# Seven products instead of eight in some block pairs of a gate and up projection, with the middle activations turned through device memory

## The chip, the cores and the metric

The kernel is one launch on one core of a Trainium2 chip. The metric is device time in microseconds, the median of several runs of the whole kernel. The engines that matter here are TensorE (PE in the profile; its weight loads are listed as PEld), VectorE (DVE), ScalarE (ACT), GpSimd (POOL) and SyncE (SP), which only issues DMAs.

## The reference

One layer of a decoder trunk on 256 tokens of width 2048, with 16 learned tokens ahead of them, in float32. The layer is a half-step FFN, a mixer of sparse attention and a gated short convolution, and a second half-step FFN, which is the part that is changed:

```python
def swiglu(x, w_gate, w_up, w_down):
    return (jax.nn.silu(x @ w_gate) * (x @ w_up)) @ w_down
...
        u = rms_norm(h, ffn2_norm_g[l])
        h = h + 0.5 * swiglu(u, ffn2_w_gate[l], ffn2_w_up[l], ffn2_w_down[l])
```

`w_gate` and `w_up` are 2048 x 5632, `w_down` is 5632 x 2048. The result is the 256 tokens without the learned ones.

## The kernel before

**Precision.** Every float32 operand of a large matmul is split into a rounded part (hi) and the rest (lo), and a product is three matmuls: hi·hi, hi·lo, lo·hi. The activations are split once and stay on chip (`act`, `mid`). Each weight is read once from device memory and split on the way.

**The stream.** `Stream` (L66 to L158) runs through all weights of the kernel in the order in which they are used. A chunk is 128 x 2048 floats, 1 MB; SyncE loads it into one of three `raw` buffers (L100). `split` (L106) cuts a chunk into subs of 1024 columns, here two blocks of 128 x 512. For each sub ACT copies `raw` to `whi` (L115) and VectorE subtracts to get `wlo` (L116). There are four buffers of each, and splits are issued three subs ahead of the one in use, so the split of a sub waits for the matmuls of the fourth sub before it. `next` (L137), called by the matmul code for each sub, first issues the split that is due, and then the steps that other code has put off with `later(fn, lag)`: these run in order of their due sub. So the order of instructions on ACT and VectorE is written out by hand, counted in subs. Each engine takes its instructions in that order.

**The second FFN.** `ffn_tokens` (L487) keeps tokens as the output rows: 128 tokens (index `j`, 1 or 2) by 512 columns is one accumulator bank. The 5632 middle columns are 11 slices of 512, in two groups of 6 and 5 (`GROUPS`). For each slice `f`:

- `tokens` (L308) makes the gate: 16 blocks of weights (`k`), two per sub, for both `j`, three matmuls each (L316 to L318): 8 subs of 12 matmuls of 128x512. Then the same for up: 192 matmuls in all.
- `gate` (L505) is Silu on ACT from the accumulator, with the norm's scale of each token; `times` (L509) multiplies by the up half on VectorE.
- `turn_columns` (L478) turns the 256 tokens x 512 columns so that columns lie on partitions: per call four VectorE transposes of 32 partitions x 256 (L389), four calls per slice, 16 transposes. A 32x32 block is turned in place by one transpose; taking a source and a target on different partitions moves the block.
- `split_into` (L339) writes hi and lo of the turned slice to `mid`.

After a group's slices come four output blocks `pd` of 512 columns each, with `mid` as activations, and `add` (L515) adds them to the residual.

Ahead of the second FFN the output projection of the mixer (`po`) makes the new residual in four quarters `g`. `add_out` (L1045) adds and squares, `turn_columns` turns, and `to_act` (L1056) scales, and splits into `act`. The last quarter falls into the first subs of the second FFN: its 16 transposes come two calls to a sub there (`per`), then `to_act`.

Of the kernel before, what the change touches and what calls it, by code (L numbers as in the profile page):

```python
# [23 lines left out]
META = 16  # L24
# [37 lines left out]
PITCH = 5 * LINE  # L62
LATER = LINE - META
SUB = 1024
RAW = 2048


class Stream:
# [7 lines left out]
    def __init__(self, nc, raw_pool, split_pool):  # L76
        self.nc, self.raw_pool, self.split_pool = nc, raw_pool, split_pool
        self.loads, self.subs = [], []
        self.raw, self.ready = {}, {}
        self.n_loaded = self.n_split = self.at = 0  # L80
        self.blocks, self.waiting, self.steps = [], [], []
        self.first = []

    def add(self, src, n, width, cuts=()):

# [20 lines left out]
    def split(self, upto):  # L106
        nc = self.nc
        while self.n_split < min(upto, len(self.subs)):
            g, c, kk, width = self.subs[self.n_split]
            self.load(g + RAW_BUFS)  # L110
            n = kk * width
            raw = self.raw[g][:, c : c + n]
            hi = self.split_pool.tile([P, SUB], F32R, name="whi")
            lo = self.split_pool.tile([P, SUB], F32R, name="wlo")
            nc.scalar.activation(hi[:, :n], raw, AF.Copy)  # L115
            nc.vector.tensor_sub(lo[:, :n], raw, hi[:, :n].bitcast(F32))  # L116
# [4 lines left out]
            if self.n_split == len(self.subs) or self.subs[self.n_split][0] > g:  # L121
                self.load(g + 1 + RAW_BUFS)

    def later(self, fn, lag=1, least=0):

# [36 lines left out]
def tile_decoder_layer(  # L162
# [22 lines left out]
    nc = tc.nc  # L185
# [26 lines left out]
    chunks(wo, 0, KD, 512)  # L212
    gu = down = 0
    for n in GROUPS:
        chunks(wgu2, gu, gu + 8 * n, 512)
        chunks(wd2, down, down + 4 * n, 512)
        gu, down = gu + 8 * n, down + 4 * n

# [53 lines left out]
    def mm_tile(name="mm"):  # L272
        return psum.tile([P, 512], F32, name=name, tag="mm")
# [34 lines left out]
    def tokens(ps_of, x, n):  # L308

        k = 0  # L310
        while k < n:
            blocks = [st.next()] + st.rest()
            for j, ps in ps_of.items():
                for i, (whi, wlo) in enumerate(blocks):
                    xhi, xlo = x(k + i, j, 0), x(k + i, j, 1)
                    nc.tensor.matmul(ps, xhi, whi, start=k + i == 0, stop=False)  # L316
                    nc.tensor.matmul(ps, xhi, wlo, start=False, stop=False)  # L317
                    nc.tensor.matmul(ps, xlo, whi, start=False, stop=k + i == n - 1)  # L318
            k += len(blocks)

    def act_tokens(k, j, part):
        t0, n = TT[j]
# [155 lines left out]
    def turn_columns(mt, s, r):  # L478

        for q in range(4):  # L480
            turned(
                mt.rearrange("p f (j r b) -> p r j f b", j=2, r=4)[:, r],
                s.rearrange("p j (f q b) -> p q j f b", f=4, q=4)[:, q],
                q, r,
            )

    def ffn_tokens():  # L487

        with tc.tile_pool(name="ffn2", bufs=1, reuse_waits="tile") as fp:
            mid = fp.tile([P, 4 * GROUPS[0], 2, SEQ], F32R, name="mid")  # L490

            late["junk"] = lambda: fp.tile([P, 512], F32, name="junk")
            late["mt"] = lambda: fp.tile([P, 4, SEQ], F32, name="mt", bufs=2)
            root, inverse = rsqrt(rcol[:, 0, :2], sums[:, 0], (P, 2), 1.0 / D)

            def add_up():
                for g in (0, 2):
                    nc.vector.tensor_add(sums[:, g], sums[:, g], sums[:, g + 1])
# [6 lines left out]
            def gate(pg, s):  # L505
                for j in (1, 2):
                    nc.scalar.activation(s[:, j - 1], pg[j], AF.Silu, scale=rcol[:, 0, j - 1 : j])

            def times(pu, s):  # L509
                for j in (1, 2):  # L510
                    nc.vector.scalar_tensor_tensor(
                        s[:, j - 1], pu[j], rcol[:, 0, j - 1 : j], s[:, j - 1], op0=ALU.mult, op1=ALU.mult
                    )

            def add(d, j, pd, last):  # L515
                to = ht[d][:, j - 1]
                nc.vector.scalar_tensor_tensor(to, pd, 0.5, to, op0=ALU.mult, op1=ALU.add)
                if last:
                    queue = nc.gpsimd if st.n_loaded < len(st.loads) else (nc.sync, nc.scalar)[j - 1]
                    queue.dma_start(out[j - 1, :, d * 512 : (d + 1) * 512], to)  # L520

            for c, n in enumerate(GROUPS):
                for f in range(n):
                    s = fp.tile([P, 2, 512], F32, name="s", bufs=2)
                    mt = fp.tile([P, 4, SEQ], F32, name="mt", bufs=2)
                    pg = {j: mm_tile(f"pg{j}") for j in (1, 2)}
                    tokens(pg, act_tokens, KD)
                    st.later(lambda pg=pg, s=s: gate(pg, s))
                    pu = {j: mm_tile(f"pu{j}") for j in (1, 2)}
                    tokens(pu, act_tokens, KD)  # L530
                    st.later(lambda pu=pu, s=s: times(pu, s))
                    for r in range(4):
                        st.later(lambda mt=mt, s=s, r=r: turn_columns(mt, s, r), 2 + r)
                    to = mid[:, 4 * f : 4 * f + 4]
                    st.later(lambda to=to, mt=mt: split_into(to[:, :, 0], to[:, :, 1], mt), 6)
# [27 lines left out]
    late = {}  # L563
    with ExitStack() as mix:
# [491 lines left out]
        def to_act(g, mt):  # L1056
            for f in range(4):
                d = 4 * g + f
                hi, lo = (act[:, d, i, LATER + META :][:, :SEQ] for i in range(2))
                gain = gains[2][:, d : d + 1]  # L1060
                nc.scalar.activation(hi, mt[:, f], AF.Copy, scale=gain)
                nc.vector.scalar_tensor_tensor(
                    lo, mt[:, f], gain, hi.bitcast(F32), op0=ALU.mult, op1=ALU.subtract
                )
# [12 lines left out]

# [67 lines left out]
def _layout(x, meta_tokens, ffn1_norm_g, ffn1_w_gate, ffn1_w_up, ffn1_w_down, mix_norm_g, w_in, q_norm_g,  # L1145
# [32 lines left out]
    gu = np.stack([_tiles(ffn2_w_gate[0], 512), _tiles(ffn2_w_up[0], 512)], 1)  # L1178
    a["wgu2"] = _chunks(gu.reshape(-1, P, KD * 512))
    a["wd2"] = _down_columns(ffn2_w_down[0])  # L1180
    return a

# [18 lines left out]
```

## Time and profile before

| | |
|---|---|
| median of 3 runs | 2143.2 us (2143.09 to 2143.22) |
| span of the profiled execution | 2141.4 us |
| first and last gate matmul of the second FFN start at | 1419.0 and 2006.4 us |
| busy: TensorE, VectorE, ACT, GpSimd | 2136.3, 1325.8, 954.5, 10.0 us |
| read from device memory | 393.49 MB |

The span runs from the first to the last instruction of one profiled execution; the runs' times are whole executions, and the profiled one's own time is known by its span alone. A row of instructions reads: source line, engine, operation, output <- inputs, shapes, count, then busy time and mean duration of one in ns, then the time in which the engine stood idle just before them and what ended it. A row of the timeline reads: start, duration, engine, line, operation, and in brackets the idle time before it. Matmuls are pipelined, so the duration of one is longer than the distance to the next.

### The profile page before, as it was taken

How to read it: one execution, taken by the hardware profiler on the slowest of the kernel's cores; microseconds unless marked ns; L12 is line 12 of the kernel's file. 1: busy time of each engine (PE TensorE's matmuls, PEld its weight loads, DVE VectorE, ACT ScalarE, POOL GpSimd, SP SyncE). 2: the span in 40 equal slices, each digit the busy share in tenths (PEclk: the TensorE clock that was granted, in tenths of full speed). 3: DMA queues.
4: the chain of work that ended last, by engine and by line, in shares of the span. 5: the costliest groups of instructions: out<-in, count | busy, mean ns of one | idle time of the engine just before them, and what ended most of it. 6: DMA issues, size and time to landing. Idle time of an engine off the chain costs nothing.

```text
span 2141.4 us, 30929 instructions
## 1 busy us (share of the span) xinstructions
PE 2136.3 (100%) x12902; PEld 1921.2 (90%) x12902; DVE 1325.8 (62%) x1776; ACT 954.5 (45%) x1173; POOL 10.0 (0%) x28
## 2 busy tenths in 40 slices
PE   9999999999999999999999999999999999999999
PEld 9999999999999998799988888888888888888887
DVE  7555544455555556677686487886676644666664
ACT  6444433344444445565444444454444433444442
POOL 0000000000000000000000000000000000000000
PEclk9999999999999999999999999999999999999999
DMA  7555545555544545454555555555555555555554
GB/s 267 189 181 179 179 180 178 178 177 177 177 178 178 177 170 177 159 176 158 172 188 194 194 189 204 177 183 210 196 196 186 196 191 195 196 197 195 189 200 143
DMA packets 56909, 397.58 MB, mean 186 GB/s; under 512 B 6337, under 2 KB 7105, under 8 KB 9409
## 3 DMA queue, kind: packets, MB, share of 16 engines
q1 hardware_dynamic: 55872, 393.51, 53.4%
q8 instruction: 101, 1.65, 0.3%
q10 hardware_dynamic: 576, 1.05, 0.1%
q0 software_dynamic: 320, 1.05, 0.1%
q14 instruction: 40, 0.32, 0.0%
HBM read 393.49 MB, written 2.10 MB: 185 GB/s over the span
## 4 chain that ended last, share of the span: by engine, by line
PE 99%; DMA 0%; DVE 0%; SPq 0%; ACT 0%; issue 0%; ACTq 0%
PE pd L290 4%; PE pd L289 4%; PE pd L288 4%; PE pu L289 4%; PE pg L289 4%; PE pg L288 4%; PE pu L288 4%; PE pu L290 4%; PE pg L290 4%; PE pg L317 4%; PE pg L318 4%; PE pd L318 4%; PE pu L317 4%; PE pg L316 4%; PE pu L316 4%; PE pd L316 4%
## 5 line engine op out<-in xcount | busy, mean ns | idle before, releaser
L116 DVE TENSOR_TENSOR wlo<-raw,whi 128x1024 fp32r<-128x1024 f32 (+1 forms) x749 | 912.7, 1220 | 780.6 <-ACT whi L115 777.6
L115 ACT ACTIVATE whi<-raw 128x1024 fp32r<-128x1024 f32 (+1 forms) x749 | 788.3, 1055 | 1079.2 <-PE pd L289 146.3
L288 PE MATMUL pd<-mid,whi 128*128 128x272 f32 x704 | 201.7, 286 | 0.0
L289 PE MATMUL pd<-mid,whi 128*128 128x272 f32 x704 | 201.7, 286 | 0.0
L290 PE MATMUL pd<-mid,wlo 128*128 128x272 f32 x704 | 201.7, 286 | 0.0
L288 PE MATMUL pu<-act,whi 128*128 128x272 f32 x672 | 192.6, 287 | 0.0
L289 PE MATMUL pu<-act,whi 128*128 128x272 f32 x672 | 192.5, 287 | 0.0
L288 PE MATMUL pg<-act,whi 128*128 128x272 f32 x672 | 192.5, 286 | 0.0
L289 PE MATMUL pg<-act,whi 128*128 128x272 f32 x672 | 192.5, 286 | 0.0
L290 PE MATMUL pg<-act,wlo 128*128 128x272 f32 x672 | 192.5, 286 | 0.0
L290 PE MATMUL pu<-act,wlo 128*128 128x272 f32 x672 | 192.5, 286 | 0.0
L317 PE MATMUL pg<-wlo,act 128*128 128x512 f32 x352 | 137.2, 390 | 0.0
L318 PE MATMUL pg<-whi,act 128*128 128x512 f32 x352 | 137.1, 389 | 0.0
L316 PE MATMUL pg<-whi,act 128*128 128x512 f32 x352 | 136.9, 389 | 0.0
L316 PE MATMUL pu<-whi,act 128*128 128x512 f32 x352 | 136.9, 389 | 0.0
L317 PE MATMUL pu<-wlo,act 128*128 128x512 f32 x352 | 136.9, 389 | 0.0
L318 PE MATMUL pu<-whi,act 128*128 128x512 f32 x352 | 136.9, 389 | 0.0
L316 PE MATMUL pd<-whi,mid 128*128 128x512 f32 x352 | 136.9, 389 | 0.0
L317 PE MATMUL pd<-wlo,mid 128*128 128x512 f32 x352 | 136.9, 389 | 0.0
L318 PE MATMUL pd<-whi,mid 128*128 128x512 f32 x352 | 136.9, 389 | 0.0
L288 PEld LDWEIGHTS pd<-mid,whi 128*128 128x128 f32 x704 | 132.6, 188 | 0.0
L289 PEld LDWEIGHTS pd<-mid,whi 128*128 128x128 f32 x704 | 132.6, 188 | 0.0
(248 smaller groups left out, 4014.3 us busy)
## 6 DMA issues: line engine op xcount, KB each, us to landing
raw<-in_wgu_dram SPq DMA_DIRECT2D x174, 1024.0 KB, 4.8
raw<-in_wd_dram SPq DMA_DIRECT2D x88, 1024.0 KB, 4.8
raw<-in_wcv_dram SPq DMA_DIRECT2D x24, 1024.0 KB, 4.8
raw<-in_wgc_dram SPq DMA_DIRECT2D x24, 1024.0 KB, 4.9
raw<-in_wga_dram SPq DMA_DIRECT2D x24, 1024.0 KB, 4.8
raw<-in_wo_dram SPq DMA_DIRECT2D x16, 1024.0 KB, 4.8
raw<-in_wqi_dram SPq DMA_DIRECT2D x8, 1024.0 KB, 4.9
raw<-in_wq_dram SPq DMA_DIRECT2D x8, 1024.0 KB, 4.8
```

Of the source, the lines that this page charges most:

```text
L115: nc.scalar.activation(hi[:, :n], raw, AF.Copy)
L116: nc.vector.tensor_sub(lo[:, :n], raw, hi[:, :n].bitcast(F32))
L288: nc.tensor.matmul(ps, whi, xhi, start=first, stop=False)
L289: nc.tensor.matmul(ps, whi, xlo, start=False, stop=False)
L290: nc.tensor.matmul(ps, wlo, xhi, start=False, stop=last)
L316: nc.tensor.matmul(ps, xhi, whi, start=k + i == 0, stop=False)
L317: nc.tensor.matmul(ps, xhi, wlo, start=False, stop=False)
L318: nc.tensor.matmul(ps, xlo, whi, start=False, stop=k + i == n - 1)
```

## The change

Gate and up are made side by side. Two blocks of activations (`k`, `k + 1`) times the four weight blocks gate/up of these two make a 2 x 2 product of blocks (two token halves by gate and up). The weights are laid out on the host so that one chunk holds these four blocks. Of the eight such pairs of a slice, pairs 3 and 5 (`MIXED`; the very first slice: pair 5 alone) are made with seven products instead of eight (Strassen's scheme in Winograd's form), the rest as before.

- The four accumulators `c[j, q]` (q: gate or up) and four more `m[1], m[5], m[6], m[7]` are all eight banks; they change places from slice to slice.
- A mixed chunk has four subs instead of two (`add_mixed`, `part`): a is two of its blocks as they are, and VectorE makes two differences besides; b is the other two, one of them now a difference, and VectorE makes a sum and a difference besides; c is two combinations; d is one. Their products number 2, 2, 2 and 1, each of three matmuls.
- The combinations of activations for the two pairs are made once, by `combos`, in the first slice.
- `spread` and `gather` add the `m` to the accumulators: one ACT copy and eight VectorE sums of 128x512 per slice, from the accumulator banks. Silu then reads from on-chip memory, and `times` too.
- Except in the last slice of each group, `turn_columns` is replaced by `turn_blocks` (two VectorE transposes of 128x512, which turn each 32x32 block in place), `move_blocks` (GpSimd's queue: one DMA of 512 KB to device memory and four of 128 KB back, which put the blocks on their partitions) and, nine subs later, `split_blocks` (two ACT copies and two VectorE subtractions of 128x512). In the last slices `turn_columns` runs two calls to a sub.
- In the mixer's last output quarter the transposes come one call to a sub, and `to_act` at the sixth sub, as in the other quarters; the norm's steps come four subs later.

The core of the diff:

```diff
@@ class Stream
+    def add_mixed(self, src):
+        g = len(self.loads)
+        self.loads.append((src, RAW, ()))
+        self.subs += [(g, part, 0, HALF) for part in "abcd"]
...
+    def part(self, raw, name):
+        sub, add = self.nc.vector.tensor_sub, self.nc.vector.tensor_add
+        b11, b12, b22, b21 = (raw[:, i * HALF : (i + 1) * HALF] for i in range(4))
+        t3, t2, t4 = (self.mix[:, i * HALF : (i + 1) * HALF] for i in range(3))
+        if name == "a":
+            sub(t3, b22, b12)
+            sub(b12, b12, b11)
+            return raw[:, 2 * HALF :]
+        if name == "b":
+            add(t2, t3, b11)
+            sub(t4, b21, t2)
+            return raw[:, : 2 * HALF]
+        return self.mix[:, : 2 * HALF] if name == "c" else t4
...
+    def quads(c, m, x, mixed, n, after_mixed):
...
+                plan.append([
+                    [(c[1, 1], s[4], 0), (c[1, 0], of(k + 1, 1), 1)],
+                    [(m[1], of(k, 1), 0), (m[5], s[1], 1)],
+                    [(m[7], s[3], 0), (m[6], s[2], 1)],
+                    [(c[2, 0], of(k + 1, 2), 0)],
+                ])
...
@@ ffn_tokens
+            def combos(n, i):
...
+                nc.vector.tensor_add(y, x[:, :, 0], x[:, :, 1])
+                nc.vector.tensor_add(z[:, 0], y[:, 0, 1], y[:, 1, 1])
+                nc.vector.tensor_sub(z[:, 1], z[:, 0], y[:, 0, 0])
+                nc.vector.tensor_sub(z[:, 2], y[:, 0, 0], y[:, 0, 1])
+                nc.vector.tensor_sub(z[:, 3], y[:, 1, 0], z[:, 1])
+                split_into(comb[:, n, :, 0], comb[:, n, :, 1], z)
...
-            st.later(add_up, 4)
-            st.later(root, 5)
-            st.later(inverse, 6)
+            st.later(add_up, 8)
+            st.later(root, 9)
+            st.later(inverse, 10)
...
+            def spread(m):
+                nc.scalar.activation(u[:, 0], m[1], AF.Copy)
+                nc.vector.tensor_add(u[:, 2], m[6], u[:, 0])
+                nc.vector.tensor_add(u[:, 1], m[7], u[:, 2])
+                nc.vector.tensor_add(u[:, 2], m[5], u[:, 2])
+                nc.vector.tensor_add(u[:, 3], m[5], u[:, 1])
+
+            def gather(c, s):
                 for j in (1, 2):
+                    nc.vector.tensor_add(s[:, j - 1], c[j, 0], u[:, j - 1])
+                for j in (1, 2):
+                    nc.vector.tensor_add(u[:, j + 1], c[j, 1], u[:, j + 1])
+                for j in (1, 2):
+                    nc.scalar.activation(s[:, j - 1], s[:, j - 1], AF.Silu, scale=rcol[:, 0, j - 1 : j])
...
+            def turn_blocks(x, s):
+                for j in range(2):
+                    nc.vector.transpose(
+                        x[:, :, j].rearrange("p q (f b) -> p f q b", f=4),
+                        s[:, j].rearrange("p (f q b) -> p f q b", q=4, f=4),
+                    )
+
+            def move_blocks(mt, x):
+                hold = hbm.tile([P, 4, 2, P], F32, name="hold")
+                nc.gpsimd.dma_start(hold, x)
+                rows = hold.rearrange("(r f) q j c -> q f r (j c)", r=4)
+                for q in range(4):
+                    nc.gpsimd.dma_start(mt[q * 32 : q * 32 + 32], rows[q])
+
+            def split_blocks(to, mt):
+                for j in range(2):
+                    x = mt[:, :, j].rearrange("p r (f b) -> p f r b", f=4)
+                    hi, lo = (to[:, :, i, j * P : (j + 1) * P].rearrange("p f (r b) -> p f r b", r=4) for i in range(2))
+                    split_into(hi, lo, x)
...
                 for f in range(n):
...
+                    if f == c == 0:
+                        st.later(lambda: combos(1, MIXED[1]), 6)
+                        st.later(lambda: combos(0, MIXED[0]), 18)
+                    now = {i: mixed[i] for i in MIXED[f == c == 0 :]}
+                    quads(cc, m, act_tokens, now, 8, lambda m=m: st.later(lambda: spread(m)))
+                    st.later(lambda cc=cc, s=s: gather(cc, s))
+                    st.later(lambda s=s: times(s), 2)
                     to = mid[:, 4 * f : 4 * f + 4]
+                    if f < n - 1:
+                        st.later(lambda xt=xt, s=s: turn_blocks(xt, s), 3)
+                        st.later(lambda mt=mt, xt=xt: move_blocks(mt, xt), 4)
+                        st.later(lambda to=to, mt=mt: split_blocks(to, mt), 13)
+                    else:
+                        mt = mt.rearrange("p r j c -> p (r j c)").rearrange("p (f t) -> p f t", f=4)
+                        for r in range(4):
+                            st.later(lambda mt=mt, s=s, r=r: turn_columns(mt, s, r), 3 + r // 2)
+                        st.later(lambda to=to, mt=mt: split_into(to[:, :, 0], to[:, :, 1], mt), 5)
...
-            per = 2 if g == 3 else 1
             for r in range(4):
-                st.later(lambda g=g, r=r, box=box: turn_columns(box["m"], ht[g], r), 2 + r // per)
-            st.later(lambda g=g, box=box: to_act(g, box["m"]), 2 + 4 // per)
+                st.later(lambda g=g, r=r, box=box: turn_columns(box["m"], ht[g], r), 2 + r)
+            st.later(lambda g=g, box=box: to_act(g, box["m"]), 6)
```

`quads` runs the products of a plan sub by sub, `trio` is the three matmuls of one product, and `s[1]` to `s[4]` are the combinations made by `combos`.

More of the change, by code (lines that the diff above doesn't have):

```diff
@@ L64 @@
 SUB = 1024
+HALF = 512
+MIXED = (3, 5)
 RAW = 2048
@@ L111, in split @@
             n = kk * width
-            raw = self.raw[g][:, c : c + n]
+            if n:
+                raw = self.raw[g][:, c : c + n]
+            else:
+                raw = self.part(self.raw[g], c)
+                n = raw.shape[1]
+                kk = n // width
             hi = self.split_pool.tile([P, SUB], F32R, name="whi")
@@ L120, in split @@
             self.n_split += 1
-            if self.n_split == len(self.subs) or self.subs[self.n_split][0] > g:
+            if self.n_split == len(self.subs) or self.subs[self.n_split][0] > g or c == "b":
                 self.load(g + 1 + RAW_BUFS)
+    def part(self, raw, name):
[11 more added lines that the diff above has]
+        return self.mix[:, : 2 * HALF] if name == "c" else t4
     def later(self, fn, lag=1, least=0):
@@ L214, in tile_decoder_layer @@
     for n in GROUPS:
-        chunks(wgu2, gu, gu + 8 * n, 512)
+        for i in range(gu, gu + 8 * n):
+            if i % 8 in MIXED[i < 8 :]:
+                st.add_mixed(wgu2[i])
+            else:
+                st.add(wgu2[i], 4, 512)
         chunks(wd2, down, down + 4 * n, 512)
@@ L319, in tokens, with trio, of @@
             k += len(blocks)
+    def trio(ps, x, w, first, last):
+        nc.tensor.matmul(ps, x(0), w[0], start=first, stop=False)
+        nc.tensor.matmul(ps, x(0), w[1], start=False, stop=False)
+        nc.tensor.matmul(ps, x(1), w[0], start=False, stop=last)
+    def quads(c, m, x, mixed, n, after_mixed):
+        def of(k, j):
+            return lambda part: x(k, j, part)
+        plan = []
+        for i in range(n):
+            k = 2 * i
+            if i in mixed:
+                s = [None, *(lambda part, q=q, i=i: mixed[i](q, part) for q in range(4))]
+                plan.append([
[4 more added lines that the diff above has]
+                ])
+            else:
+                plan.append([
+                    [(c[j, q], of(k + u, j), q ^ u) for j in (1, 2) for q in ((0, 1), (1, 0))[u]] for u in range(2)
+                ])
+        flat = [id(p[0]) for steps in plan for unit in steps for p in unit]
+        at = 0
+        for i, units in enumerate(plan):
+            for unit in units:
+                blocks = [st.next()] + st.rest()
+                for ps, xx, b in unit:
+                    trio(ps, xx, blocks[b], id(ps) not in flat[:at], id(ps) not in flat[at + 1 :])
+                    at += 1
+            if i == max(mixed):
+                after_mixed()
     def act_tokens(k, j, part):
@@ L487, in ffn_tokens @@
     def ffn_tokens():
-        with tc.tile_pool(name="ffn2", bufs=1, reuse_waits="tile") as fp:
+        with ExitStack() as pools:
+            fp = pools.enter_context(tc.tile_pool(name="ffn2", bufs=1, reuse_waits="tile"))
+            hbm = pools.enter_context(tc.tile_pool(name="hold", bufs=2, space=bass.MemoryType.DRAM))
             mid = fp.tile([P, 4 * GROUPS[0], 2, SEQ], F32R, name="mid")
-            late["junk"] = lambda: fp.tile([P, 512], F32, name="junk")
+            st.mix = fp.tile([P, 3 * HALF], F32, name="mix")
+            u = fp.tile([P, 4, 512], F32, name="u")
+            comb = fp.tile([P, len(MIXED), 4, 2, P], F32R, name="comb")
+            mixed = {i: lambda q, part, n=n: comb[:, n, q, part] for n, i in enumerate(MIXED)}
+            late["junk"] = lambda: u[:, 0]
+            def combos(n, i):
+                y = st.mix[:, :HALF].rearrange("p (b j t) -> p b j t", b=2, j=2)
+                z = st.mix[:, HALF : 2 * HALF].rearrange("p (q t) -> p q t", q=4)
+                x = act[:, 2 * i : 2 * i + 2, :, LATER + META :].bitcast(F32).rearrange("p b i (j t) -> p b i j t", j=2)
+                nc.vector.tensor_add(y, x[:, :, 0], x[:, :, 1])
[4 more added lines that the diff above has]
+                split_into(comb[:, n, :, 0], comb[:, n, :, 1], z)
             late["mt"] = lambda: fp.tile([P, 4, SEQ], F32, name="mt", bufs=2)
@@ L499, in add_up @@
                 nc.vector.tensor_add(sums[:, 0], sums[:, 0], sums[:, 2])
-            st.later(add_up, 4)
-            st.later(root, 5)
-            st.later(inverse, 6)
-            def gate(pg, s):
-                for j in (1, 2):
-                    nc.scalar.activation(s[:, j - 1], pg[j], AF.Silu, scale=rcol[:, 0, j - 1 : j])
-            def times(pu, s):
+            st.later(add_up, 8)
[7 more added lines that the diff above has]
+                nc.vector.tensor_add(u[:, 3], m[5], u[:, 1])
@@ L510, in times @@
+            def gather(c, s):
+                for j in (1, 2):
+                    nc.vector.tensor_add(s[:, j - 1], c[j, 0], u[:, j - 1])
[3 more added lines that the diff above has]
+                    nc.scalar.activation(s[:, j - 1], s[:, j - 1], AF.Silu, scale=rcol[:, 0, j - 1 : j])
+            def times(s):
                 for j in (1, 2):
                     nc.vector.scalar_tensor_tensor(
-                        s[:, j - 1], pu[j], rcol[:, 0, j - 1 : j], s[:, j - 1], op0=ALU.mult, op1=ALU.mult
+                        s[:, j - 1], u[:, j + 1], rcol[:, 0, j - 1 : j], s[:, j - 1], op0=ALU.mult, op1=ALU.mult
@@ L515, in add, with banks @@
+            def split_blocks(to, mt):
[3 more added lines that the diff above has]
+                    split_into(hi, lo, x)
+            def banks():
+                one, two, x = mm_tile("one"), mm_tile("two"), aux_tile("three")
+                return [x[:, 0], x[:, 1], one, two]
             def add(d, j, pd, last):
@@ L523, in ffn_tokens @@
                 for f in range(n):
-                    s = fp.tile([P, 2, 512], F32, name="s", bufs=2)
+                    s = fp.tile([P, 2, 512], F32, name="s")
                     mt = fp.tile([P, 4, SEQ], F32, name="mt", bufs=2)
[L526 to L530, printed above, removed]
@@ L531, in ffn_tokens @@
-                    st.later(lambda pu=pu, s=s: times(pu, s))
-                    for r in range(4):
-                        st.later(lambda mt=mt, s=s, r=r: turn_columns(mt, s, r), 2 + r)
-                    to = mid[:, 4 * f : 4 * f + 4]
-                    st.later(lambda to=to, mt=mt: split_into(to[:, :, 0], to[:, :, 1], mt), 6)
+                    xt = fp.tile([P, 4, 2, P], F32, name="xt", bufs=1)
+                    mt = fp.tile([P, 4, 2, P], F32, name="mt", bufs=2)
+                    sides = banks(), banks()
@@ new lines, in ffn_tokens @@
+                    main, side = sides[f % 2], sides[1 - f % 2]
+                    cc = {(j, q): main[2 * j - 2 + q] for j in (1, 2) for q in range(2)}
+                    m = dict(zip((1, 5, 6, 7), side))
+                    if f == c == 0:
[3 more added lines that the diff above has]
+                    quads(cc, m, act_tokens, now, 8, lambda m=m: st.later(lambda: spread(m)))
@@ new lines, in ffn_tokens @@
+                    st.later(lambda cc=cc, s=s: gather(cc, s))
+                    st.later(lambda s=s: times(s), 2)
+                    to = mid[:, 4 * f : 4 * f + 4]
+                    if f < n - 1:
+                        st.later(lambda xt=xt, s=s: turn_blocks(xt, s), 3)
+                        st.later(lambda mt=mt, xt=xt: move_blocks(mt, xt), 4)
+                        st.later(lambda to=to, mt=mt: split_blocks(to, mt), 13)
+                    else:
+                        mt = mt.rearrange("p r j c -> p (r j c)").rearrange("p (f t) -> p f t", f=4)
+                        for r in range(4):
+                            st.later(lambda mt=mt, s=s, r=r: turn_columns(mt, s, r), 3 + r // 2)
+                        st.later(lambda to=to, mt=mt: split_into(to[:, :, 0], to[:, :, 1], mt), 5)
@@ L536, in ffn_tokens @@
+                if n % 2:
+                    mm_tile(), mm_tile()
                 for d in range(D // 512):
@@ L1177, in _layout @@
     a["wo"] = _chunks(_tiles(w_out[0], 512))
-    gu = np.stack([_tiles(ffn2_w_gate[0], 512), _tiles(ffn2_w_up[0], 512)], 1)
-    a["wgu2"] = _chunks(gu.reshape(-1, P, KD * 512))
+    g, u = (_tiles(w[0], 512).reshape(FF // 512, P, KD // 2, 2, 512) for w in (ffn2_w_gate, ffn2_w_up))
+    gu = np.stack([g[:, :, :, 0], u[:, :, :, 0], u[:, :, :, 1], g[:, :, :, 1]], 3).transpose(0, 2, 1, 3, 4)
+    a["wgu2"] = np.ascontiguousarray(gu).reshape(-1, P, RAW)
     a["wd2"] = _down_columns(ffn2_w_down[0])
```

## Prediction

> **What bounds the kernel now.** I read the page first: the busy shares and the chain that ended last; then the clock.
>
> ```profile
> span 2141.4 us, 30929 instructions
> PE 2136.3 (100%) x12902; PEld 1921.2 (90%) x12902; DVE 1325.8 (62%) x1776; ACT 954.5 (45%) x1173; POOL 10.0 (0%) x28
> ...
> PE 99%; DMA 0%; DVE 0%; SPq 0%; ACT 0%; issue 0%; ACTq 0%
> ```
> ```profile
> core 0: 2141.4 us, clock 1.000
> ```
>
> TensorE is busy from end to end at the full granted clock, and the chain is its matmuls. Second, the waits of TensorE:
>
> ```profile
> PE warm L281 <- POOL ones L240: 1.0, 1, 1.0
> PE start L290 <- DVE wlo L116: 0.2, 1, 0.2
> PE start L288 <- ACT whi L115: 0.2, 1, 0.2
> ```
>
> Nearly no waiting: there is nothing to win but matmuls that need not run, and everything to lose by starving the engine. The span is 2141.4; the median of the runs is 2143.2, so 1.8 us lie around the span. I take them as constant and add the differences to the median.
>
> **The price of a matmul.** The tile view gives the first and last start of gate matmuls in the second FFN:
>
> ```profile
> L316 PE MATMUL pg<-whi,act x352: 388/389/397, 1419.0 to 2006.4; 128*128 128x512 f32 x176
> ```
>
> Between these starts lie eleven stages of 192 less the last stage's up half (96), plus the first down projection (4·2·24·3 = 576), less 3: 2589 matmuls in 587.4 us, 0.2269 each. The 389 ns are latency, since matmuls overlap. That includes small stalls; within a stage the timeline gives 12 matmuls (one sub, the two blocks split at once) per 2.72 us, the pitch at which ACT's splits come, or 0.2267 each:
>
> ```profile
> 1455.10 1.06 ACT L115 ACTIVATE whi<-raw 128x1024 fp32r<-128x1024 f32 x1 [1.66 <-PE pu L318]
> ...
> 1456.19 1.23 DVE L116 TENSOR_TENSOR wlo<-raw,whi 128x1024 fp32r<-128x1024 f32 x1 [1.49 <-ACT whi L115]
> ...
> 1457.82 1.06 ACT L115 ACTIVATE whi<-raw 128x1024 fp32r<-128x1024 f32 x1 [1.66 <-PE pu L318]
> ```
>
> ACT and VectorE (DVE) each rest more than half of this period, waiting for TensorE to free a buffer.
>
> **What is removed.** An ordinary pair of blocks takes 2 token halves × 2 outputs × 2 blocks = 8 products of 3 matmuls; a mixed pair takes 7. The first stage has one mixed pair, the ten others two each: 21 products, 63 matmuls. 63 × 0.2267 = **14.3 us** off the path, if TensorE stays fed. A stage (one turn of the `f` loop) falls from 192 to 186 matmuls, 42.2 us. [...]
>
> **What is added on VectorE.** Rows for the prices:
>
> ```profile
> L116 DVE TENSOR_TENSOR wlo<-raw,whi 128x1024 fp32r<-128x1024 f32 x741 | 906.9, 1226 | 777.7 <-ACT whi L115 774.8
> L115 ACT ACTIVATE whi<-raw 128x1024 fp32r<-128x1024 f32 x741 | 783.0, 1059 | 1073.6 <-PE pd L289 146.3 <-PE pu L289 139.3 <-PE pg L289 137.2
> L389 DVE STREAM_TRANSPOSE mt<-s 32x256 f32<-32x256 f32 x176 | 76.7, 436 | 2.8
> L511 DVE SCALAR_TENSOR_TENSOR s<-pu,rcol,s 128x512 f32<-128x512 f32 x22 | 15.4, 744 | 0.0
> L507 ACT ACTIVATE s<-pg,rcol 128x512 f32<-128x512 f32 x22 | 13.8, 676 | 0.0
> L1047 DVE TENSOR_TENSOR first<-po,first 128x512 f32<-128x512 f32 x8 | 5.1, 683 | 0.0
> L116 DVE TENSOR_TENSOR wlo<-raw,whi 128x512 fp32r<-128x512 f32 x6 | 4.1, 691 | 0.9 <-ACT whi L115 0.9
> L115 ACT ACTIVATE whi<-raw 128x512 fp32r<-128x512 f32 x6 | 3.7, 622 | 2.2 <-DMA raw<-in_wgu_dram 2.1
> L594 DVE TENSOR_TENSOR zk<-zk,small 128x256 f32<-128x256 f32 x2 | 0.8, 420 | 0.0
> L594 DVE TENSOR_TENSOR zk<-zk,small 32x256 f32<-32x256 f32 x1 | 0.4, 404 | 0.0
> L605 DVE TENSOR_TENSOR rot<-zz,rope 128x128 f32<-128x128 f32 x4 | 1.1, 287 | 0.1
> ```
>
> A mixed pair's parts a and b each bring two 512-wide sums and a 1024-wide split (2.61 us), c a split (1.23), d half a split (0.69): 7.13 us, against 2.45 for an ordinary pair and against 21 × 0.2267 = 4.76 us of TensorE. A stage with two mixed pairs then asks of VectorE: 12 ordinary splits 14.7; mixed 14.3; `spread` and `gather` 8 × 0.683 = 5.5; `times` 1.5; two whole transposes; the split of the turned tile in two halves 1.4. No row has a 128x512 transpose. The two L594 rows say that time goes by elements per partition, not by partitions, so I take 0.69 each; the other bound is that the sixteen of today (16 × 0.436 = 7.0 us) are merely joined and cost the same. With 0.69 the sum is 38.7 of 42.2 us: VectorE comes close to being the bound but is not.
>
> The sum is not enough, because the load comes in bursts. A sub's split waits for the buffer of the fourth sub before it, so it must finish while three subs run. The tightest place is the first sub after the second mixed pair. Count from TensorE's start of the sub ahead of that pair, when VectorE has just ended a: it then does b (2.6), c (3.8), d (4.5), the two halves of the turned tile (5.9), the wanted split (7.1). TensorE needs its low part at 2.72 + 4.76 + 0.23 = 7.7. Margin 0.6 us; the cost per stage is nothing while no operation is more than some 8% dearer, and is bounded by a few tenths above that (5 us in all). The second narrow place is the entry of each down projection, where the last stage still turns by columns: about 18.6 us of VectorE work fall in five subs (13.6 us), against some 6 us of lead. I take nothing for it; a bound is 1 us.
>
> ACT has 12 × 1.06 for the ordinary splits, 2 × 3.8 for the mixed, and 3.2 for one copy, two halves and two Silu: 23.5 of 42.2 us.
>
> Two new waits cost nothing by this count. `gather` waits for the stage's last matmul, but so does the buffer of the split queued just ahead of it. And the eight accumulators of a stage take all banks, so the next stage's first products wait for `spread`: it comes after three more splits, at 7.1 + 3.7 + 2.7 = 13.5 on the count above, and the stage ends at 18.4.
>
> **The first stage.** This is where I expect a loss. Today TensorE is already late there, since VectorE turns and scales the last quarter of the residual; three starts 0.39 and 0.34 apart instead of 0.227 lose 0.3 us:
>
> ```profile
> 1435.62 0.49 PE L317 MATMUL pg<-wlo,act 128*128 128x512 f32 x1
> 1436.01 0.50 PE L318 MATMUL pg<-whi,act 128*128 128x512 f32 x1
> 1436.35 0.39 PE L316 MATMUL pg<-whi,act 128*128 128x512 f32 x1
> ```
>
> The change spreads that quarter's turns over four subs, as the third quarter's are today, and pair 6 needs the result only at the 15th sub, so this wait goes. But `combos` falls due in the same call as `to_act`. The third quarter, whose subs start at 1419.0 − 21.8 + 2.72 n, shows what it joins:
>
> ```profile
> 1415.14 1.22 DVE L116 TENSOR_TENSOR wlo<-raw,whi 128x1024 fp32r<-128x1024 f32 x1
> 1416.28 1.67 DVE L1062 SCALAR_TENSOR_TENSOR act<-mt,small,act 128x256 fp32r<-128x256 f32 x4
> 1417.87 2.36 DVE L116 TENSOR_TENSOR wlo<-raw,whi 128x1024 fp32r<-128x1024 f32 x2
> ...
> 1437.06 0.23 DVE L498 TENSOR_TENSOR sums<-sums 128x2 f32<-128x2 f32 x2
> ...
> 1438.54 0.16 DVE L375 TENSOR_SCALAR rs_v<-sums 128x2 f32<-128x2 f32 x1
> ```
>
> `to_act` ends at 1417.9. `combos` adds 0.69 + 4 × 0.287 to 1419.8, waits for ACT's copy (0.6), then 0.69 more; ACT's next split stands behind that copy, so the split of sub 9 ends near 1422.7, where TensorE wants it at 1421.9. Then a and b (2.6 each), c (1.2) and the nine tiny norm operations (about 1.2, by the last two rows) end at 1430.4, and TensorE wants c's low part at 1427.4. That is 3.0 late by durations; back to back they overlap by about 0.09 (2.36 for two splits), which gives back 0.9. I take **2.5 us** lost, with bounds 1 and 5. After it come ordinary subs, where VectorE catches up.
>
> **The moved block.** Turning goes from sixteen VectorE operations to two and five DMAs of GpSimd: 512 KB out, then four of 128 KB back that wait for it. Nothing like it runs today; nearest are:
>
> ```profile
> raw<-in_wgu_dram SPq DMA_DIRECT2D x174, 1024.0 KB, 4.8
> ...
> out_dram<-first POOLq DMA_DIRECT2D x4, 256.0 KB, 5.3
> ...
> out_dram<-first ACTq DMA_DIRECT2D x2, 256.0 KB, 4.1
> ```
> ```profile
> L520 POOL DMA_DIRECT2D out_dram<-first x4 | 2.3, 583 | 1013.5 <-issue 987.8 <-DVE first L517 25.6
> ```
>
> Size hardly counts (1 MB lands as fast as 256 KB), so: write 6, four issues 2.3, last landing 5.3: 13.7 us. Bounds: 9 (landings of 4.1, as from ACT's queue, and one issue) to 26.5 (all five one after another, 5.3 each). I take the value from GpSimd's own row.
>
> Its cover: from the stage's start VectorE does a split behind ACT's (2.3), `gather` (2.7), waits for ACT's next copy behind the Silu (1.1), a split (1.2), `times` (1.5), a split (1.2) and the two transposes (1.4): 11.4 us. TensorE reaches the sub after pair 5 at 8 × 2.72 + 2 × 4.76 = 31.3. Ahead of it must go two ACT halves and that sub's two splits (0.6 + 0.6 + 1.1 + 1.2, less the 0.23 by which the low part may come later). 31.3 − 11.4 − 3.3 = **16.6 us**. ACT is in order: if the tile is late, the weight splits queued behind `split_blocks` wait, and TensorE after them. At 13.7 it costs nothing. On GpSimd's queue stand only these DMAs until the outputs at the end. On SP's, loads get 1 MB per stage as company to their 8; the load that follows part b of pair 5 has the least time, 10.2 − 2.6 = 7.6 us on the count above, and 4.8 is needed.
>
> **Sum.** 2143.2 − 14.3 + 2.5 − 0.3 = **2131.1 us**.
>
> **Rivals.** [...] Chance 0.10.
>
> *VectorE becomes the bound*: if the transposes keep today's 7.0 us, the stage asks 44.3 of 42.2 us, 2.1 × 9 = 19 us, 2150; if instead ACT's copy in part a waits for the sums in the same tile, or the sums cost a tenth more, some 0.5 per stage, 2136. For it: the margin of 0.6. Against: the L594 rows, and the overlap, which the durations above do not count. Chance 0.10, of which 0.06 for the smaller sizes.
>
> [...] Chance 0.03.
>
> **Numbers.** Forecast 0.77, alone 2128.6 (no new loss) to 2135. The range 2128.6 to 2138 takes in the third rival and the smaller sizes of the second; what is left out is the late tile, the dear transposes and single mishaps, about 0.17. A measurement tells about 0.2%, 4.3 us, from no change. Faster than 2138.9: 0.77 + 0.06 + 0.03 = 0.86; within: 0.04, from a slightly late tile or half the dear transposes; slower than 2147.5: 0.10.
>
> **What would show it.** Right: 63 matmuls fewer, pitch 0.227, waits of TensorE for `wlo` only near the first stage and 2 to 3 us long in sum; transposes of 128x512 near 0.7; VectorE near 90% busy per stage; the four reads landing 14 us after `turn_blocks`. Wrong: TensorE waiting at the same place of each stage, for `whi` behind a late `mt` (late tile) or for `wlo` (VectorE), or a pitch above 0.23.

## The result, and the profile after

The changed kernel takes 2132.39 us (median of 4 runs, 2131.99 to 2132.57) against 2143.21 for the kernel before in the same session: 10.8 us less, a ratio of 0.9948 with an interval of 0.9934 to 0.9962. The forecast was 2131.1.

The page of the changed kernel: the span, the busy shares, and the chain that ended last by engine.

```profile
span 2130.8 us, 31133 instructions
...
PE 2123.0 (100%) x12839; PEld 1909.7 (90%) x12839; DVE 1418.4 (67%) x1885; ACT 995.8 (47%) x1237; POOL 34.8 (2%) x73
...
PE 97%; DVE 1%; DMA 1%; ACT 0%; issue 0%; SPq 0%; ACTq 0%
```

There are 63 matmuls fewer (12902 to 12839). VectorE has 93 us more of work in all, GpSimd 25 us. The chain is still TensorE's, but 1% each of VectorE and of DMAs has come into it. The waits of TensorE say how much (who waited for what: us in total, times, longest):

```profile
PE three L355 <- DVE wlo L129: 1.5, 3, 0.8
...
PE two L355 <- DVE wlo L129: 0.8, 1, 0.8
```

Before, the second FFN had no wait that this view lists. The ledger comes from the tile view, first start of a gate matmul and last start of the last output matmul. After, then before:

```profile
L354 PE MATMUL three<-whi,act x310: 388/389/397, 1419.5 to 2016.1; 128*128 128x512 f32 x155
```
```profile
L350 PE MATMUL pd<-whi,mid x352: 388/389/389, 1677.2 to 2126.7; 128*128 128x512 f32 x176
```
```profile
L318 PE MATMUL pd<-whi,mid x352: 388/389/389, 1681.1 to 2137.4; 128*128 128x512 f32 x176
```

From 1419.0 to 2137.4 were 718.4 us, from 1419.5 to 2126.7 are 707.2: 11.2 less. The removed matmuls account for 63 × 0.2267 = 14.3, so 3.1 us more are lost than before. The remaining 0.4 lies ahead of the change: the second FFN started at 1419.5 instead of 1419.0, and in all profiles of this study that start varies between 1418.8 and 1420.6. In sum 14.3 − 3.1 − 0.4 = 10.8; the spans of the two profiles differ by 10.6, since 0.2 more pass behind the last of these matmuls.

All of the 3.1 us is lost in one place. The timeline of TensorE in the first stage of the changed kernel (start, duration):

```profile
1443.93 0.39 PE L354 MATMUL three<-whi,act 128*128 128x512 f32 x1
1444.76 0.50 PE L355 MATMUL three<-wlo,act 128*128 128x512 f32 x1 [0.44 <-DVE wlo L129]
...
1448.79 0.39 PE L354 MATMUL three<-whi,act 128*128 128x512 f32 x1
1450.02 0.50 PE L355 MATMUL three<-wlo,act 128*128 128x512 f32 x1 [0.85 <-DVE wlo L129]
...
1451.29 0.50 PE L354 MATMUL two<-whi,comb 128*128 128x512 f32 x1
1452.55 0.50 PE L355 MATMUL two<-wlo,comb 128*128 128x512 f32 x1 [0.76 <-DVE wlo L129]
```

Read the distances of starts, not the brackets, since a duration of 0.39 hides part of a wait: 0.83, 1.23 and 1.26 instead of 0.227. With the smaller gaps behind them (0.34 where 0.23 is due, and one of 0.57) the stage loses 3.5 us, where the kernel before lost 0.4 in the same way. In the ten other stages and both output parts no two matmuls start more than 0.26 apart.

What VectorE did there (bracket: idle time before the instruction, and what ended it):

```profile
1440.09 0.68 DVE L572 TENSOR_TENSOR mix<-act 128x512 f32<-128x512 f32 x1
...
1442.53 0.69 DVE L409 TENSOR_TENSOR comb<-mix,comb 128x512 fp32r<-128x512 f32 x1 [0.70 <-ACT comb L408]
1443.48 1.23 DVE L129 TENSOR_TENSOR wlo<-raw,whi 128x1024 fp32r<-128x1024 f32 x1 [0.26 <-ACT whi L128]
...
1449.88 0.16 DVE L443 TENSOR_SCALAR rs_v<-sums 128x2 f32<-128x2 f32 x1
1451.27 1.23 DVE L129 TENSOR_TENSOR wlo<-mix,whi 128x1024 fp32r<-128x1024 f32 x1 [1.22 <-ACT whi L128]
```
```profile
1450.08 0.20 ACT L444 ACTIVATE rs_z<-rs_v 128x2 f32<-128x2 f32 x1 [1.57 <-DVE rs_v L443]
```

VectorE, which is late here, twice stands idle: 0.96 us while ACT copies `comb` and then the next split, and 1.22 us where ACT waited for `rs_v` to take the root (1.57 us idle itself) and only afterwards copied part c.

A row of the windows view gives a stretch and its length, then the busy time (and number of instructions) of TensorE, its loads, VectorE, ACT and GpSimd, then the granted clock, the DMA share and GB/s. First the crowded stretch of the first stage, then a steady stage of after and one of before:

```profile
1435.00:1456.00 21.00, 18.78 (x79) 13.98 (x78) 18.41 (x36) 12.15 (x17) 0.00 (x0) 1.00 0.44 150
```
```profile
1520.98:1563.14 42.16, 42.16 (x187) 34.92 (x186) 36.28 (x43) 22.91 (x25) 2.75 (x5) 1.00 0.66 226
```
```profile
1560.00:1603.52 43.52, 43.52 (x194) 36.04 (x193) 28.87 (x36) 19.08 (x19) 0.00 (x0) 1.00 0.56 193
```

VectorE is busy 88% of the crowded stretch, 86% of a steady stage now, and 66% of one before. The tightest split, that of the sub after the second mixed pair, against the matmul that needs it, in the third stage:

```profile
1537.52 1.23 DVE L129 TENSOR_TENSOR wlo<-raw,whi 128x1024 fp32r<-128x1024 f32 x1
```
```profile
1539.60 0.39 PE L355 MATMUL three<-wlo,act 128*128 128x512 f32 x1
```

It ends at 1538.74, 0.86 us before its use. The block that moves through device memory, in the same stage, and the landing times of its DMAs:

```profile
1517.17 1.29 DVE L614 STREAM_TRANSPOSE xt<-s 128x512 f32<-128x512 f32 x2
```
```profile
1518.76 0.56 POOL L621 DMA_DIRECT2D hold<-xt  x1 [32.74 <-DVE xt L614]
1525.00 2.19 POOL L624 DMA_DIRECT2D mt<-hold  x4 [5.68 <-PE one L356]
```
```profile
hold<-xt POOLq DMA_DIRECT2D x9, 512.0 KB, 4.9
mt<-hold POOLq DMA_DIRECT2D x36, 128.0 KB, 5.2
```
```profile
DMA to landing us min/median/max: 4.7/5.1/7.8
```
```profile
1535.40 1.14 ACT L408 ACTIVATE mid<-mt 128x512 fp32r<-128x512 f32 x2
```

The two rows with sizes end in the median landing time; the row below them has the extremes, writes and reads together. The transposes end at 1518.46 and the last read is issued at 1526.6. The four reads of this stage are the slow ones of the trace, 7.7 to 7.8 us each: the last lands at 1534.3, 15.9 us after the transposes. ACT comes for the tile at 1535.4, only 1.1 us later. In the other eight stages the way takes 12.2 to 14.6 us, and ACT comes 2.4 us or more after the last landing. Why these four reads were slow isn't shown. (The releaser "PE one" is an inference of the view; in the other eight stages it names the write, `hold<-xt`.)

### The profile page after: what moved, and what is told of

Read it like the earlier page. It is cut to its first block, busy times and chain, and to the rows that moved or that the text cites. A ratio compares the mean times of both kernels' runs of the same rounds, so it can differ in the third digit from the quotient of the medians.

```text
span 2130.8 us, 31133 instructions
## 1 busy us (share of the span) xinstructions
PE 2123.0 (100%) x12839; PEld 1909.7 (90%) x12839; DVE 1418.4 (67%) x1885; ACT 995.8 (47%) x1237; POOL 34.8 (2%) x73
## 4 chain that ended last, share of the span: by engine, by line
PE 97%; DVE 1%; DMA 1%; ACT 0%; issue 0%; SPq 0%; ACTq 0%
PE pd L322 4%; PE pd L320 4%; PE pd L321 4%; PE pg L321 4%; PE pu L321 4%; PE pu L322 4%; PE pg L322 4%; PE pg L320 4%; PE pu L320 4%; PE pd L349 4%; PE pd L348 4%; PE pd L350 4%; PE three L355 3%; PE three L356 3%; PE three L354 3%; PE pgt L350 3%
## 5 line engine op out<-in xcount | busy, mean ns | idle before, releaser
L322 PEld LDWEIGHTS pd<-mid,wlo 128*128 128x128 f32 x704 | 132.6, 188 | 0.0
L320 PEld LDWEIGHTS pu<-act,whi 128*128 128x128 f32 x672 | 126.6, 188 | 0.0
L321 PEld LDWEIGHTS pg<-act,whi 128*128 128x128 f32 x672 | 126.6, 188 | 0.0
L322 PEld LDWEIGHTS pg<-act,wlo 128*128 128x128 f32 x672 | 126.6, 188 | 0.0
L320 PEld LDWEIGHTS pg<-act,whi 128*128 128x128 f32 x672 | 126.6, 188 | 0.0
L321 PEld LDWEIGHTS pu<-act,whi 128*128 128x128 f32 x672 | 126.6, 188 | 0.0
```

What stands on the lines that cost most here:

```text
L320: nc.tensor.matmul(ps, whi, xhi, start=first, stop=False)
L321: nc.tensor.matmul(ps, whi, xlo, start=False, stop=False)
L322: nc.tensor.matmul(ps, wlo, xhi, start=False, stop=last)
```

## The experiments

The theory after the result (A): TensorE pays the same price for every product, and the only loss is a VectorE queue in the first stage, made of `combos` and of the norm's detour over ACT. Rivals: the mixed pair's dear splits alone; a cost in every stage; and, from the prediction, the late tile and VectorE as the next bound. The experiments belong to three later sessions, in which the kernel before took 2143.66 us (the first four below), 2143.53 (the last) and 2143.28 (the others) against 2143.21 above; so a distance to the changed kernel's 2132.39 is uncertain by some 0.5 us.

**The norm's steps later.**

```diff
-            st.later(add_up, 8)
-            st.later(root, 9)
-            st.later(inverse, 10)
+            st.later(add_up, 15)
+            st.later(root, 16)
+            st.later(inverse, 17)
```

> The changed kernel with one edit: the three steps of the norm (add_up, root, inverse) fall due at the 15th to 17th sub of the first stage instead of the 8th to 10th, still ahead of the first Silu. Theory A: the 3.5 us that TensorE loses in the first stage come from VectorE's queue there, and about 2 us of them from the norm: its nine small operations (1.2 us) and the 1.2 us in which VectorE stands idle while ACT waits for the sum, takes the root and only then copies part c. Expected loss 1.5 us instead of 3.5, time about 2130.4. Rival B (the loss is combos alone, which stands ahead of it): loss stays near 3.5, time 2132.4.

Measured: 2130.38 us.

```profile
PE three L355 <- DVE wlo L129: 1.0, 2, 0.5
```

The three long gaps are two now (0.82 and 0.93 between starts), with 1.5 us lost in the first stage. A small gap of 0.41 has come up in the second stage, at its first mixed pair, which makes 1.8 us in all. The moved norm now stands just ahead of the second call of `combos`; that this makes VectorE late there is read from the order of instructions, not tested. The rest is as A has it.

**`combos` earlier.**

```diff
-                        st.later(lambda: combos(1, MIXED[1]), 6)
+                        st.later(lambda: combos(1, MIXED[1]), 1)
```

> The changed kernel with one edit: combos of pair 5 falls due at the first sub of the first stage, where VectorE waits for ACT, instead of at the sixth together with to_act. Theory A: 2.5 us of VectorE work and its wait for ACT leave the crowded stretch, so the loss of TensorE falls from 3.5 to about 1.3 us, time about 2130.2. Rival C (the loss belongs to the mixed pair's own dear splits, not to what precedes them): the loss stays above 3, time about 2132.

Measured: 2130.34 us.

```profile
PE two L355 <- DVE wlo L129: 0.7, 1, 0.7
```

The two first gaps are gone, the third (1.12, behind the root) stays: 1.5 us lost. Rival C falls: the mixed pair's own splits are the same in this run.

**Both edits.**

> Both edits together. Theory A: the two causes add up, nothing else is late; TensorE loses 0 to 0.5 us in the first stage and the time is the pure saving, 2143.2 - 14.3 + 0.3 = about 2129.2. If a third cause is there, 1 us or more stays, 2130 or above.

Measured: 2129.38 us, ratio 0.9933 (0.9920 to 0.9947). That is 14.3 us less than the kernel before in the same session, the price of the 63 matmuls. The waits view lists nothing in the second FFN any more:

```profile
PE warm L313 <- POOL ones L272: 1.0, 1, 1.0
PE start L322 <- DVE wlo L129: 0.2, 1, 0.2
```

The distances of starts still show one gap of 0.40 and one of 0.34, 0.3 us, both in the second stage. In the first stage nothing is lost any more: its loss is explained in full.

**`split_blocks` too early: the late tile, made.**

```diff
-                        st.later(lambda to=to, mt=mt: split_blocks(to, mt), 13)
+                        st.later(lambda to=to, mt=mt: split_blocks(to, mt), 8)
```

> The changed kernel with one edit: split_blocks falls due at the 8th sub after its slice instead of the 13th, so ACT reaches it while the four reads are still under way. This tests the late tile that was a rival. Theory: ACT is in order, the weight splits behind it wait, and TensorE after them; the turned tile lands about 13 us after turn_blocks, ACT would come to it some 8 us after, and about 3 us of that are not covered by the subs split ahead: 9 x 3 = 27 us slower, about 2159. Rival: the subs split ahead cover it, time unchanged at 2132.4.

Measured: 2167.90 us, 35.5 more than the changed kernel; 27 were expected. ACT waits for the tile in all nine stages, and TensorE for ACT:

```profile
ACT mid L408 <- DMA mt<-hold: 37.3, 9, 5.6
```
```profile
PE three L354 <- ACT whi L128: 11.9, 9, 2.7
PE three L355 <- DVE wlo L129: 10.4, 16, 0.9
```

The gaps between starts add up to 27 us over the nine stages, as expected. The other 8 us are something else: after five of the nine waits the matmuls come 0.427 apart for a while. The windows view of such a stretch, and of the 4.5 us behind it:

```profile
1494.00:1497.20 3.20, 3.20 (x9) 2.50 (x8) 3.16 (x5) 1.71 (x2) 0.00 (x0) 0.52 0.91 294
1497.50:1502.00 4.50, 4.50 (x21) 3.71 (x21) 4.09 (x5) 2.94 (x5) 0.00 (x0) 0.99 0.57 191
```

The granted clock is 0.52 there (the third column from the right), with TensorE busy throughout: 9 matmuls where 14 would fit.

**`split_blocks` only a little too early.** The same edit with 10 in place of 13.

> The changed kernel with split_blocks due at the 10th sub after its slice (13th in the changed kernel, 8th in the run that cost 35 us). The turned tile lands about 13 us after turn_blocks; ACT would reach it about 2 us early and the next copy, of part b, would come about 1.6 us late, where VectorE has the two sums of part b to do meanwhile and a margin of 0.6 to 1 us. Theory (a wait costs only what is beyond the cover, and the granted clock stays full for such a short stall): 0 to 1 us per stage, 2132.4 to 2141, no stretch of matmuls 0.43 us apart. Rival (any wait of ACT for the tile stops TensorE by as much): 9 x 2 us or more, 2150.

Measured: 2134.48 us, 2.1 more than the changed kernel (1.4 by the starts of the matmuls), and no slow stretch. ACT waits for the tile in all nine stages, 13.1 us in sum. For its 2.9 us in the second stage TensorE loses 1.0, for its 2.3 in the third, shown here, 0.4, and in the other seven, where ACT waits 0.9 to 1.6, nothing.

```profile
1532.62 1.16 ACT L408 ACTIVATE mid<-mt 128x512 fp32r<-128x512 f32 x2 [2.30 <-DMA mt<-hold]
```

So most of a wait is covered by the subs split ahead, and the rival falls.

**All slices turned by columns.**

```diff
-                    if f < n - 1:
+                    if f < 0:
```

> The changed kernel with one edit: all slices turn by columns on VectorE, sixteen transposes, two calls to a sub, and nothing goes through device memory. In the changed kernel VectorE was busy 36.3 of 42.16 us in a stage; this adds 7.0 - 1.4 = 5.6 us and takes nothing away, 41.8 of 42.2. Theory (the turn through device memory is what leaves VectorE room for the mixed pairs): the sum just fits but the bursts do not, TensorE waits for wlo in each of the nine stages, 1 to 3 us each, time 2141 to 2160, so most or all of the gain is lost. Rival (the move to GpSimd's DMAs is worth nothing): 2132.4, with waits in the first stage only.

Measured: 2184.97 us, ratio 1.0195 (1.0181 to 1.0209): 52.6 more than the changed kernel, beyond the 9 to 28 expected, and slower than the kernel before. The rival falls more plainly than the theory was right. TensorE's longest waits, then VectorE in the fourth stage:

```profile
PE three L355 <- DVE wlo L129: 33.8, 13, 4.6
```
```profile
1572.07 3.57 DVE L457 STREAM_TRANSPOSE mt<-s 32x256 f32<-32x256 f32 x8
...
1578.26 3.59 DVE L457 STREAM_TRANSPOSE mt<-s 32x256 f32<-32x256 f32 x8
...
1583.21 1.22 DVE L129 TENSOR_TENSOR wlo<-raw,whi 128x1024 fp32r<-128x1024 f32 x1
```

Two bursts of eight transposes stand ahead of the dear splits of parts a and b. The split of b, which ends at 1584.4, is the one that TensorE waits for: its starts are 3.81 apart there. Behind seven of the nine such waits the clock is halved again, for 3.4 us or, twice, for 6.8:

```profile
1585.50:1588.90 3.40, 3.32 (x8) 2.11 (x8) 3.40 (x5) 1.06 (x1) 0.00 (x0) 0.51 0.78 292
```

In that stage the wait costs 3.7 us and the slow stretch 1.9; over the nine stages it is 36.7 and 15.0 us. The expectation had neither the second nor the full size of the first, because it reasoned from a sum (41.8 of 42.2 us) and not from the burst. A wider spread of the sixteen transposes over the subs was not tried, so the run prices this placing and not every way to turn on VectorE.

**One mixed pair instead of two.**

```diff
-MIXED = (3, 5)
+MIXED = (5,)
...
-            if i % 8 in MIXED[i < 8 :]:
+            if i % 8 in MIXED:
...
-                        st.later(lambda: combos(1, MIXED[1]), 6)
-                        st.later(lambda: combos(0, MIXED[0]), 18)
-                    now = {i: mixed[i] for i in MIXED[f == c == 0 :]}
+                        st.later(lambda: combos(0, MIXED[0]), 6)
+                    now = {i: mixed[i] for i in MIXED}
```

> The changed kernel with one mixed pair (pair 5) in every slice instead of two: 11 products less than the kernel before instead of 21, 33 matmuls x 0.2267 = 7.5 us. Theory: the price of a product is the same everywhere and the rest of the change costs only what the first stage loses, 3.5 us against 0.4 before; time 2143.4 - 7.5 + 3.1 = about 2139.0. If the second pair cost something in each stage, this one would come nearer than 6.8 us to the changed kernel's 2132.4.

Measured: 2139.27 us (11 runs), ratio 0.9980 (0.9972 to 0.9989). That is 6.9 us above the changed kernel for 30 matmuls more, 6.8 expected. The second pair costs nothing beside what it saves.

**Three mixed pairs.** On the kernel with both steps moved:

```diff
-MIXED = (3, 5)
+MIXED = (2, 4, 6)
...
+                        st.later(lambda: combos(1, MIXED[1]), 1)
-                        st.later(lambda: combos(0, MIXED[0]), 18)
+                        st.later(lambda: combos(0, MIXED[0]), 17)
+                        st.later(lambda: combos(2, MIXED[2]), 18)
...
-                        st.later(lambda to=to, mt=mt: split_blocks(to, mt), 13)
+                        st.later(lambda to=to, mt=mt: split_blocks(to, mt), 16)
```

> The kernel with both steps moved (2129.4) with three mixed pairs in a slice (pairs 2, 4 and 6; the first slice: pair 4 alone), one buffer less for the turned tile to make room, and split_blocks at the 16th sub. 10 products less, 30 matmuls x 0.2267 = 6.8 us, if TensorE stays fed: 2122.6. But VectorE, busy 36.3 of 42.2 us with two pairs, gets 4.7 more: 41.0 of 41.5 us. Theory (VectorE is the next bound): it can't absorb the bursts, TensorE waits for wlo in every stage, and most of the 6.8 us are lost: 2126 to 2132. Rival (VectorE has room to the last): 2122.6.

Measured: 2133.91 us, inside neither 2126 to 2132 nor 2122.6. Where it was lost tells more than the sum:

```profile
PE three L355 <- DVE wlo L129: 5.2, 3, 2.4
PE three L354 <- DVE u L596: 1.3, 8, 0.2
```

The three waits for `wlo` are in the first two stages, some 8 us there, with a slow stretch at a clock of 0.54. In the first stage VectorE has `to_act` between the sums of parts a and b of the mixed pair; in the second it comes from two calls of `combos`. In the eight later stages that follow a mixed one TensorE waits only 0.4 us each by its starts, for the last sum of `spread`, which frees the bank that the next stage wants first. No steady stage waits for a split: the theory that VectorE can't take the bursts falls.

**Three mixed pairs, with these waits taken away.**

```diff
-                    now = {i: mixed[i] for i in (MIXED[1:2] if f == c == 0 else MIXED)}
+                    now = {} if f == c == 0 else mixed
...
-                        st.later(lambda: combos(0, MIXED[0]), 17)
-                        st.later(lambda: combos(2, MIXED[2]), 18)
+                        st.later(lambda: combos(0, MIXED[0]), 12)
+                        st.later(lambda: combos(2, MIXED[2]), 14)
...
-                    m = dict(zip((1, 5, 6, 7), side))
+                    m = dict(zip((6, 7, 1, 5), side))
```

The first slice takes Silu and product straight from the accumulators.

> Three mixed pairs (2, 4 and 6) again, with what the run before lost taken away: the first slice has no mixed pair (its Silu and product read the accumulators), the three calls of combos fall due at its 1st, 12th and 14th sub, the norm's steps at the 8th to 10th, and m6 and m7 lie in the banks that the next slice wants first, so that spread frees those first. 30 products less than the kernel before: 90 matmuls x 0.2267 = 20.4 us. Theory: VectorE can carry three pairs in the steady state (the run before waited 0.4 us per slice there, for spread alone), and its 11 us of lost time came from the crowded first two slices and from spread; 2143.3 - 20.4 + 0 to 2 = 2123 to 2125. Rival (VectorE at 41 of 41.5 us is full, and the waits come back elsewhere, for wlo): 2128 or more, no better than 2129.4 with two pairs.

Measured: 2122.57 us, ratio 0.9902 (0.9885 to 0.9918): 21.0 us less than the kernel before in the same session, 9.8 less than the changed kernel, and just under the 2123 to 2125 expected. The waits of TensorE, and a steady stage:

```profile
PE warm L313 <- POOL ones L272: 1.0, 1, 1.0
PE start L320 <- ACT whi L128: 0.3, 1, 0.3
```
```profile
1563.14:1604.60 41.46, 41.46 (x184) 34.34 (x183) 40.20 (x49) 24.63 (x28) 2.74 (x5) 1.00 0.67 228
```

VectorE is busy 40.20 of 41.46 us, 97%, and TensorE waits for nothing in the second FFN; no two starts there are over 0.26 apart. The edits were made together, so what each gave back is read from the waits of the run before, not shown one by one.

## Why the prediction was right, point by point

The forecast of 2131.1 us was 1.3 too low. The ledger splits this into 1.0 us more lost in the first stage, 0.4 ahead of the second FFN, which no term had, and 0.1 the other way, since the old loss that went was 0.4 and not 0.3.

- *63 matmuls, 0.2267 us each, off the path.* Right: counted on the page, priced by the ledger, and confirmed from the other side by the run with one pair (6.9 us for 30).
- *VectorE close to the bound, but not the bound.* Right. The count by durations was 38.7 us of a stage, measured 36.3, since operations back to back overlap: two whole transposes take 1.29 us together. One takes 0.686 us, against 0.69 taken.
- *The tightest split has 0.6 us to spare.* Right in place and nearly in size: 0.86.
- *The moved block takes 13.7 us of a cover of 16.6.* Right as a typical value: 12.2 to 14.6 us in eight stages. The cover was 16.9. But the third stage took 15.9, because its reads landed after 7.7 to 7.8 us where the prediction counted 5.3, and so the late tile was 1.1 us away there. The mechanism of the late tile is real (ACT waits 37.3 us for it with `split_blocks` at 8, 13.1 at 10); only its condition isn't met. The chance of 0.10 for a late tile was the author's estimate, and no run shows it come from GpSimd: with VectorE 86% busy its issues took 0.55 to 0.58 us each, but for 0.71 of the very first write.
- *The first stage loses 2.5 us, and the 0.3 of before go.* The mechanism was right, the size too small: it loses 3.5, and before it was 0.4. The prediction's own count came to 3.0 − 0.9 = 2.1 and was rounded up to 2.5 without a reason, which happened to go the right way. The count had VectorE's work for the norm (1.2 us) but not the 1.2 us in which VectorE stands idle because ACT waits for `rs_v` before it copies part c. That is about the size of what was missing. Moving the norm alone cut the loss in all to 1.8; it moved the work and the idle time together, so their shares are not shown apart.
- *VectorE becomes the bound* was a rival for dear transposes. Its price for that case was 19 us in nine stages; the run that has them lost 52.6. The price was made from the sum of a stage, and the bursts and the clock were left out.
- *The matmuls removed bring less* was the third rival, with a chance of 0.03: no run shows a price for a switch of accumulator. A steady stage takes 42.16 us for its 186 matmuls, 0.2267 each as before, with the accumulators alternating every three.

## What to carry to other kernels

A product taken out of this matmul-bound stream was worth its matmuls (6.9 us for 30, 6.8 by their pitch), as long as the engine that prepares operands kept up. Whether it does is told by running its queue in order from one deadline to the next, not by its share of busy time: at 97% busy nothing was lost in the steady stages of the last run, and 3.5 us were lost in the changed kernel's first stage, in a stretch at 88%, where two round trips between VectorE and ACT stood in a crowded stretch. So place the detours over another engine, however tiny, where there is slack, and let the buffer that is wanted first be freed first.

## What the runs showed of the hardware

A wait of TensorE can cost more than its length. In three runs (`split_blocks` at 8, all slices by columns, and the first with three pairs) matmuls came 0.427 us apart instead of 0.227 though TensorE was busy again: 8 of the 35 us lost with `split_blocks` at 8, and 1.9 of the 5.6 in a stage turned by columns. There are thirteen such stretches in the second FFN: five, seven and one in these runs. In windows that lie on one, in the same order, the granted clock is 0.52 (1494.00 to 1497.20), 0.51 (1585.50 to 1588.90) and 0.54 (1480.50 to 1484.00). The mean granted clocks of the runs, 0.996, 0.993 and 0.999 over 2165.6, 2182.5 and 2131.3 us, come to about 17, 31 and 4 us at half speed. With two of the seven twice as long as the rest that is some 3.4 us for each, an estimate from these rounded clocks.

Not every wait was followed by half speed. Two stages of the run with `split_blocks` at 8 show it. Gaps of 1.59 and 1.26 us between starts came ahead of a window at 0.56 (1585.85 to 1589.60). In the next stage gaps of 1.81 and 1.26 came ahead of one at 1.00 (1632.80 to 1636.30). The changed kernel's first stage, with gaps of 0.83, 1.23 and 1.26, kept its clock (1.00 from 1435 to 1456), and so did the second stage with `split_blocks` at 10, with a gap of 1.10 (1.00 from 1480 to 1520). So the sum of a stage's gaps does not tell which waits are followed by half speed: the larger one was not. What decides was not shown.
